# Layer 0 with six combined chunks, tile 2's chunks all behind them, and tile 1's pooling not held

## The chip, the cores and the metric

The kernel runs on one core of a Trainium2 chip. TensorE multiplies matrices, VectorE and ScalarE work element by element, and SyncE (SP) issues nearly all DMA transfers. The metric is the time of one execution on the device, in microseconds; a lower one is better.

## What is computed

One step of a streaming encoder of two layers, for a prompt of 1024 frames and a sample of 32 frames that share the weights, all in 32-bit floating point. Of the reference this matters here:

```python
for i in range(DEPTH):                                   # DEPTH = 2
    mod = jax.nn.silu(c) @ w_ada[i] + b_ada[i]
    sh1, sc1, gt1, sh2, sc2, gt2 = jnp.split(mod[:, None, :], N_MOD, axis=-1)
    h = rmsnorm(x, g_norm[i, 0]) * (1 + sc1) + sh1
    ...                                                  # layer 0: gated MLP, layer 1: pooling over time
    x = x + gt1 * rmsnorm(mix, g_norm[i, 1])
    h = rmsnorm(x, g_norm[i, 2]) * (1 + sc2) + sh2
    f = jnp.square(jax.nn.relu(h @ ffn_w_up[i])) @ ffn_w_down[i]
    x = x + gt2 * rmsnorm(f, g_norm[i, 3])
```

`ffn_w_up` is 1024 x 4096 and `ffn_w_down` 4096 x 1024 in each layer.

## The kernel before

**Tiles and chunks.** The 1056 frames are three tiles: tiles 0 and 1 of 384 frames, and tile 2 of 256 frames of the prompt and the 32 of the sample. The channel MLP of a layer is cut into eight chunks of 512 hidden channels. For one chunk and one tile (a tile-chunk) there are four up products of 24 matmuls and eight down products of 12: each product runs as three matmuls, high times high, high times low and low times high, because weights and activations are split into a high and a low part. A weight arrives through one of three raw buffers (`RAW_SLOTS`), 512 KB at a time; ScalarE makes its high part (line 436) and VectorE the low part.

**Passes.** The list `passes` (lines 322 to 333) sets the order: each entry names a layer, a chunk, and the tiles that use the weights loaded for it. In layer 0 it is: chunks 6 and 7 on tile 0; chunk 0 on tiles 0 and 1; chunk 1 on tile 0; chunk 1 on tile 1; chunks 2 to 5 combined; chunks 6 and 7 on tiles 1 and 2; chunks 0 to 5 on tile 2. In layer 1 it is: chunks 0 to 2 on tile 0; chunk 3 on tiles 0 and 1; chunks 0 to 2 on tile 1; chunks 4 to 7 combined; all eight chunks on tile 2.

**Combined chunks.** `combined_item` treats tiles 0 and 1 together and needs seven products in place of eight for a block of two by two up products. For that it uses sums and differences of the weights (`do_s`, VectorE work on `scratch`, a part of tile 2's `acc`) and of the activations' columns (`sums_of_columns`). The latter run once for a layer, need the modulated rows of all three tiles stored (`md`) and keep their results in the places of tile 0's and tile 2's `hh` and `hl` and in free buffers. So tile 2 must be modulated before the combined run, gives up its places for the length of it, and gets its rows back at the end (`late_modulation`, line 1859: ScalarE writes `hh`, VectorE `hl`). Some of the borrowed pieces hold hidden activations until the last down product of the run.

**Fillers.** All that stands between the matrix products (norms, residuals, modulation, pooling) is written as generators in the list `fillers`, named `ffn0_t`, `ffn1_t` and so on. `weave` (line 744) puts steps of them between the products as long as a running estimate of VectorE's time is behind TensorE's; `pull` (line 715) takes the first of the first two fillers that is open. A step that yields True is sticky: the same filler goes on next. A step that yields a number closes its filler for so many microseconds of the estimate. `open_` (line 719) also keeps `ffn1_1`, tile 1's pooling, closed while `ffn1_0`, tile 0's, is still in the list. The pooling groups of one tile are tied by `yield g != 3` (line 2014). Before a tile's first chunk of a layer its filler is finished by force. The framework then orders the instructions of each engine by their dependencies and an estimate of its own.

**The conditioning weights.** `w_ada` comes in items of 512 KB in the same stream as the other weights. VectorE multiplies each by the conditioning vectors and adds up (`aa`), four instructions of 512 columns for an item, and after every fourth item transposes and reduces. `some_ada` sets how many items go behind each pass: 40 of them are spread over the MLP, 4 + 2 + 2 before the combined run of layer 0, 6 behind each of its four combined chunks, 4 + 2 behind tile 2's chunks 0 and 1, and 2 behind the first combined chunk of layer 1.

Of the kernel before, what the change touches and what calls it, by code (L numbers as in the profile page):

```python
# [26 lines left out]
TILES = [(0, 384, 0), (384, 384, 0), (768, 256, DEC)]  # L27
NT = len(TILES)
W_SLOTS = 16
COMBINED = [range(2, 6), range(4, 8)]  # L30
RAW_SLOTS = 3
WINDOWS = (2, 4, 8, 16)

# [2 lines left out]
def tile_stream_encoder_step(  # L36
# [137 lines left out]
    def t_x(name, shape):  # L174
        return small.tile(shape, F32, tag="x3", bufs=3, name=name)
# [110 lines left out]
    def w_chunk(n):  # L286
        l, c, _ = passes[n]
        if n in combined:
            for i in range(2):
                f0 = c * 512 + i * 256  # L290
                for q in range(2):
                    stream.append(
                        (
                            "s",
                            ("up", n, i, q),
                            ffn_w_up[l][q * 512 : (q + 1) * 512, f0 : f0 + 256].rearrange(
                                "(k p) f -> p k f", p=P
                            ),
                            (4, 256),
                        )  # L300
                    )
        for j in range(0 if n in combined else 4):
            f = 4 * c + j
            add_w(
                ("up", n, j),
                ffn_w_up[l][:, f * P : (f + 1) * P].rearrange("(k p) f -> p k f", p=P),
                (8, P),
            )
        for q in range(4):
            add_w(  # L310
                ("dn", n, q),
                ffn_w_down[l][c * 512 : (c + 1) * 512, q * 256 : (q + 1) * 256].rearrange(
                    "(j p) d -> p j d", p=P
                ),
                (4, 256),
            )
# [3 lines left out]
    every = list(range(NT))  # L320
    pair = every[:-1]
    passes = []
    runs = []
    for l, cs in enumerate(COMBINED):
        before = [[(l, c, [0]) for c in (6, 7)] + [(l, 0, pair), (l, 1, [0]), (l, 1, [1])]]
        before.append([(l, c, [0]) for c in range(3)] + [(l, 3, pair)])
        before[1] += [(l, c, [1]) for c in range(3)]
        after = [[(l, c, every[1:]) for c in (6, 7)] + [(l, c, [NT - 1]) for c in range(6)]]
        after.append([(l, c, [NT - 1]) for c in range(8)])
        passes += before[l]  # L330
        runs.append(range(len(passes), len(passes) + len(cs)))
        passes += [(l, c, pair) for c in cs]
        passes += after[l]
# [9 lines left out]
    combined = [n for r in runs for n in r]  # L343
# [3 lines left out]
    def some_ada(n):  # L347
        for _ in range(min(n, len(rest))):
            add, l, j = rest.pop(0)
            add(l, j)  # L350
# [27 lines left out]
    for n, (l, c, tiles) in enumerate(passes):  # L378
        w_chunk(n)
        if n in combined:  # L380
            some_ada(2 if l else 6)
        elif l == 0 and c < 2:
            some_ada(4 if c == 0 else 2)
    assert not rest

    worder = [s[1] for s in stream if s[0] in "ws"]
# [323 lines left out]
    fillers = deque()  # L710
# [4 lines left out]
    def pull(force=False):  # L715

        def open_(f):
            if f[0] == "ffn1_1" and not force and any(g[0] == "ffn1_0" for g in fillers):  # L720
                return False
            return force or gates.get(f[0], 0.0) <= time["pe"]

        if sticky:
            f = sticky[-1]
            if not open_(f):
                return False
            sticky.pop()
        else:
            f = next((f for f in list(fillers)[:2] if open_(f)), None)  # L730
            if f is None:
                return False
        try:
            step = next(f[1])
        except StopIteration:
            fillers.remove(f)
            return True
        if step is True:
            sticky.append(f)
        elif step is not False:  # L740
            gates[f[0]] = max(time["pe"], time["dve"]) + step
        return True
# [1151 lines left out]
    def to_pool(st):  # L1894
        t = st.t
        n = ncol[t]
        npr, nsm = TILES[t][1], TILES[t][2]

        def run():
# [70 lines left out]
            for src, w, dst0, nm in parts:  # L1970
                for g in range(4):
                    cur = src[:, 2 * g : 2 * g + 2, :]
                    lo = 0
                    step = 1
                    for lev in range(g + 1):
                        nxt = t_x(f"win{t}{nm}{g}_{lev}", [P, 2, HALO + w])
                        lo += step
                        tt(
                            out=nxt[:, :, lo:],
                            in0=cur[:, :, lo:],  # L1980
                            in1=cur[:, :, lo - step : HALO + w - step],
                            op=ALU.add,
                        )
                        cur = nxt
                        step *= 2
                        yield True
                    body = cur[:, :, HALO:]
                    hsrc = src[:, 2 * g : 2 * g + 2, HALO:]
                    dst = acc[t][:, 2 * g : 2 * g + 2, HALO + dst0 : HALO + dst0 + w]
                    win = WINDOWS[g]  # L1990
                    first = t == 0
                    if first:
                        tt(
                            out=cur[:, :, HALO : HALO + win],
                            in0=cur[:, :, HALO : HALO + win],
                            in1=inv[:, 0:win].unsqueeze(1).broadcast_to([P, 2, win]),
                            op=ALU.mult,
                        )
                        tt(
                            out=dst[:, :, 0:win],  # L2000
                            in0=cur[:, :, HALO : HALO + win],
                            in1=hsrc[:, :, 0:win],
                            op=ALU.subtract,
                        )
                    o = win if first else 0
                    stt(
                        out=dst[:, :, o:],
                        in0=body[:, :, o:],
                        scalar=1.0 / win,
                        in1=hsrc[:, :, o:],  # L2010
                        op0=ALU.mult,
                        op1=ALU.subtract,
                    )
                    yield g != 3

            sp = Stat(t, f"rp_{t}")
            for g in range(4):
# [17 lines left out]
            yield from mix_to_ffn(sp, 1)  # L2035

        fillers.append((f"ffn1_{t}", run()))

    def run_ffn(l, after):
# [135 lines left out]
```

## Time and profile before

| | |
|---|---|
| median of 3 runs | 2147.0 us (2145.63 to 2147.81) |
| the profiled execution | 2145.2 us, span 2143.4 us |
| granted TensorE clock, mean | 0.999 |
| TensorE, matmuls / weight loads | 99% / 95% of the span busy |
| VectorE / ScalarE | 72% / 47% busy |
| channel MLP of layer 0 | 619 to 1365 us |
| combined run of layer 0 / of layer 1 | 834.7 to 1090.9 us / 1668.7 to 1921.5 us |

The page divides the span by engine, by slice and by line; TensorE's weight loads (PEld) overlap its matmuls (PE). The windows view gives the busy time of each engine in a stretch, with the number of instructions in brackets, then the granted clock (PEclk), the share of the DMA engines and their rate. Waits are put down to what came last.

### The profile page before, as it was taken

How to read it: one execution, taken by the hardware profiler on the slowest of the kernel's cores; microseconds unless marked ns; L12 is line 12 of the kernel's file. 1: busy time of each engine (PE TensorE's matmuls, PEld its weight loads, DVE VectorE, ACT ScalarE, POOL GpSimd, SP SyncE). 2: the span in 40 equal slices, each digit the busy share in tenths (PEclk: the TensorE clock that was granted, in tenths of full speed). 3: DMA queues.
4: the chain of work that ended last, by engine and by line, in shares of the span. 5: the costliest groups of instructions: out<-in, count | busy, mean ns of one | idle time of the engine just before them, and what ended most of it. 6: DMA issues, size and time to landing. Idle time of an engine off the chain costs nothing.

```text
span 2143.4 us, 33175 instructions
## 1 busy us (share of the span) xinstructions
PE 2120.2 (99%) x13041; PEld 2043.8 (95%) x13041; DVE 1533.1 (72%) x2786; ACT 1011.7 (47%) x1772; POOL 15.3 (1%) x34
## 2 busy tenths in 40 slices
PE   9999999999999999999999999999999999999998
PEld 6778999999999999999999999999999999999998
DVE  6787747466878668897778778969578654578464
ACT  5534322233456255244545556665355443365454
POOL 0000000000000000000000000000000000001000
PEclk9999999999999999999999999999999999999999
DMA  8487524353537454343434576665265322158662
GB/s 309 147 264 211 167 85 128 93 156 103 171 98 239 129 157 131 109 128 118 157 110 132 162 213 201 194 189 169 85 192 156 99 70 59 55 160 232 149 202 77
DMA packets 366002, 321.88 MB, mean 150 GB/s; under 512 B 39731, under 2 KB 328027, under 8 KB 365845
## 3 DMA queue, kind: packets, MB, share of 16 engines
q1 hardware_dynamic: 365172, 318.87, 48.8%
q8 instruction: 102, 1.67, 0.3%
q0 software_dynamic: 640, 0.88, 0.1%
q14 instruction: 56, 0.45, 0.1%
q10 hardware_dynamic: 32, 0.01, 0.0%
HBM read 279.22 MB, written 40.49 MB: 149 GB/s over the span
## 4 chain that ended last, share of the span: by engine, by line
PE 87%; DVE 5%; DMA 5%; ACT 2%; issue 1%; SPq 0%; DVEq 0%; ACTq 0%
PE pg L947 10%; PE pg L946 10%; PE pg L948 10%; PE pf L946 6%; PE pf L947 6%; PE pf L948 6%; PE pf_0a L1610 3%; PE po L947 3%; PE po L946 3%; PE po L948 3%; PE pu L946 3%; PE pu L948 3%; PE pu L947 3%; PE pv L974 2%; PE pv L973 2%; PE pv L975 2%
## 5 line engine op out<-in xcount | busy, mean ns | idle before, releaser
L946 PE MATMUL pg<-fh,wh_dn 128*128 128x384 f32 (+1 forms) x1344 | 431.6, 322 | 1.3 <-ACT fh L1359 1.1
L947 PE MATMUL pg<-fl,wh_dn 128*128 128x384 f32 (+1 forms) x1344 | 428.5, 319 | 0.9 <-DVE fl L80 0.9
L948 PE MATMUL pg<-fh,wl_dn 128*128 128x384 f32 (+1 forms) x1344 | 428.2, 319 | 0.0
L946 PE MATMUL pf<-hh,wh_up 128*128 128x288 f32 (+1 forms) x1024 | 323.2, 316 | 3.8 <-ACT wh_up L436 2.6
L947 PE MATMUL pf<-hl,wh_up 128*128 128x288 f32 (+1 forms) x1024 | 321.9, 315 | 0.8 <-DVE hl L80 0.8
L948 PE MATMUL pf<-hh,wl_up 128*128 128x288 f32 (+1 forms) x1024 | 322.1, 315 | 0.0
L946 PEld LDWEIGHTS pg<-fh,wh_dn 128*128 128x128 f32 x1344 | 252.1, 188 | 5.0 <-ACT fh L1359 3.4
L947 PEld LDWEIGHTS pg<-fl,wh_dn 128*128 128x128 f32 x1344 | 252.2, 188 | 2.2 <-DVE fl L80 1.1
L948 PEld LDWEIGHTS pg<-fh,wl_dn 128*128 128x128 f32 x1344 | 252.2, 188 | 0.0
L80 DVE TENSOR_TENSOR acc<-acc,pg 128x384 f32<-128x384 f32 (+1 forms) x336 | 172.4, 517 | 86.2 <-PE pg L948 85.3
L80 DVE TENSOR_TENSOR wl_dn<-raw,wh_dn 128x1024 fp32r<-128x1024 f32 x144 | 175.8, 1221 | 64.9 <-ACT wh_dn L436 60.3
L80 DVE TENSOR_TENSOR wl_up<-raw,wh_up 128x1024 fp32r<-128x1024 f32 (+1 forms) x160 | 160.3, 1008 | 77.6 <-ACT wh_up L436 66.3
L80 DVE SCALAR_TENSOR_TENSOR aa<-raw,csil,aa 128x512 f32<-128x512 f32 (+1 forms) x364 | 205.8, 624 | 11.6 <-DMA raw<-in_w_ada_dram 11.5
L436 ACT ACTIVATE wh_dn<-raw 128x1024 fp32r<-128x1024 f32 x144 | 151.4, 1055 | 96.8 <-PE pg L947 48.3
L946 PEld LDWEIGHTS pf<-hh,wh_up 128*128 128x128 f32 x1024 | 192.0, 188 | 5.0 <-ACT wh_up L436 3.1
L947 PEld LDWEIGHTS pf<-hl,wh_up 128*128 128x128 f32 x1024 | 192.2, 188 | 1.3 <-DVE hl L80 1.0
L948 PEld LDWEIGHTS pf<-hh,wl_up 128*128 128x128 f32 x1024 | 192.5, 188 | 0.3 <-DVE wl_up L80 0.2
L436 ACT ACTIVATE wh_up<-raw 128x1024 fp32r<-128x1024 f32 x112 | 118.3, 1058 | 134.9 <-PE pf L947 80.3
L946 PE MATMUL pu<-hh,wh_u 128*128 128x384 f32 (+1 forms) x384 | 125.8, 328 | 0.0
L946 PE MATMUL po<-ush,wh_o 128*128 128x384 f32 (+1 forms) x384 | 123.6, 322 | 0.0
L948 PE MATMUL pu<-hh,wl_u 128*128 128x384 f32 (+1 forms) x384 | 123.4, 321 | 0.0
L947 PE MATMUL pu<-hl,wh_u 128*128 128x384 f32 (+1 forms) x384 | 123.3, 321 | 0.0
(453 smaller groups left out, 4130.5 us busy)
## 6 DMA issues: line engine op xcount, KB each, us to landing
raw<-in_ffn_w_up_dram SPq DMA_DIRECT2D x144, 512.0 KB, 4.4
raw<-in_ffn_w_down_dram SPq DMA_DIRECT2D x144, 512.0 KB, 3.6
raw<-in_w_ada_dram SPq DMA_DIRECT2D x96, 512.0 KB, 4.7
raw<-in_sgu_w_in_dram SPq DMA_DIRECT2D x40, 512.0 KB, 4.2
xd<-acc SPq DMA_DIRECT2D x8, 1536.0 KB, 7.6
raw<-in_sgu_w_out_dram SPq DMA_DIRECT2D x24, 512.0 KB, 3.9
xo_r<-xd SPq DMA_DIRECT2D x32, 384.0 KB, 3.4
vd<-vt SPq DMA_DIRECT2D x32, 256.0 KB, 4.4
```

What stands on the lines that cost most here:

```text
L80: return op(out, *args, **kw)
L436: act(out=wh, in_=r, func=AF.Copy)
L946: mm(ps[:, :n], wh, rh, start=i == 0, stop=False)
L947: mm(ps[:, :n], wh, rl, start=False, stop=False)
L948: mm(ps[:, :n], wl, rh, start=False, stop=i == last)
L973: mm(ps[:m, :], a_h, wh[:, o : o + 512], start=k == 0, stop=False)
L974: mm(ps[:m, :], a_h, wl[:, o : o + 512], start=False, stop=False)
L975: mm(ps[:m, :], a_l, wh[:, o : o + 512], start=False, stop=k == KB - 1)
L1610: mm(ps[:, :n], u, v, start=first and k == 0 and x == 0, stop=k == 3 and x == 2, skip_group_check=True,)
```

## The change

Layer 0's combined run becomes chunks 2 to 7, six chunks. Ahead of it stand chunks 0 and 1 on tile 0, then chunks 0 and 1 on tile 1, each a pass with weights of its own: four tile-chunks where there were six. Behind it stand all eight chunks of tile 2, so tiles 0 and 1 both end with the combined run. There is one pass more (18 for 17). The `w_ada` items go 6 behind each of the first five combined chunks of layer 0, 2 behind the sixth, and 2 behind each of the four combined chunks of layer 1; none stands elsewhere in the MLP. Tile 1's pooling is no longer kept closed while tile 0's goes on, and a tile's pooling groups are no longer tied together.

```diff
-COMBINED = [range(2, 6), range(4, 8)]
+COMBINED = [range(2, 8), range(4, 8)]
...
-        before = [[(l, c, [0]) for c in (6, 7)] + [(l, 0, pair), (l, 1, [0]), (l, 1, [1])]]
+        before = [[(l, c, [t]) for t in pair for c in (0, 1)]]
...
-        after = [[(l, c, every[1:]) for c in (6, 7)] + [(l, c, [NT - 1]) for c in range(6)]]
+        after = [[(l, c, [NT - 1]) for c in range(8)]]
...
         if n in combined:
-            some_ada(2 if l else 6)
-        elif l == 0 and c < 2:
-            some_ada(4 if c == 0 else 2)
+            some_ada(2 if l else 6 if n + 1 in combined else 2)
...
         def open_(f):
-            if f[0] == "ffn1_1" and not force and any(g[0] == "ffn1_0" for g in fillers):
-                return False
             return force or gates.get(f[0], 0.0) <= time["pe"]
...
-                    yield g != 3
+                    yield False
```

## The prediction

> **What bounds the kernel now.** I read the page first.
>
> ```profile
> span 2143.4 us, 33175 instructions
> PE 2120.2 (99%) x13041; PEld 2043.8 (95%) x13041; DVE 1533.1 (72%) x2786; ACT 1011.7 (47%) x1772; POOL 15.3 (1%) x34
> PE 87%; DVE 5%; DMA 5%; ACT 2%; issue 1%; SPq 0%; DVEq 0%; ACTq 0%
> ```
>
> TensorE works nearly throughout and carries 87% of the chain that ended last. Fewer matmuls therefore shorten the run, unless something makes them wait. The question is what each removed matmul costs now, and which waits come in its place. So next I cut the span into its stages with the windows view: one stretch of two ordinary tile-chunks, the four combined chunks of layer 0, and the second and third combined chunk of layer 1.
>
> ```profile
> core 0: us, PE busy (x) PEld busy (x) DVE busy (x) ACT busy (x) POOL busy (x), PEclk, DMA share, GB/s
> 704.00:771.00 67.00, 67.00 (x389) 67.00 (x388) 42.37 (x72) 25.11 (x43) 0.00 (x0) 1.00 0.45 135
> 834.60:899.00 64.40, 63.63 (x368) 62.55 (x369) 54.94 (x101) 26.81 (x47) 0.00 (x0) 1.00 0.39 122
> 899.00:962.30 63.30, 63.30 (x370) 62.53 (x369) 52.26 (x92) 26.02 (x46) 0.00 (x0) 1.00 0.35 110
> 962.30:1027.20 64.90, 63.93 (x370) 62.62 (x369) 52.38 (x95) 26.02 (x46) 0.00 (x0) 1.00 0.39 122
> 1027.20:1090.90 63.70, 63.40 (x362) 62.44 (x361) 49.14 (x80) 33.17 (x66) 0.00 (x0) 1.00 0.50 156
> 1732.70:1795.40 62.70, 62.70 (x362) 62.44 (x361) 34.42 (x63) 25.11 (x46) 0.00 (x0) 1.00 0.23 68
> 1795.40:1858.20 62.80, 62.80 (x362) 62.54 (x361) 34.52 (x64) 25.11 (x46) 0.00 (x0) 1.00 0.23 68
> ```
>
> In the first row weight loads fill the whole stretch: 388 in 67.00 us, 172.7 ns for each 384-wide matmul. So I measure lost time in a row as its length less its PEld time: 1.85, 0.77, 2.28 and 1.26 us in layer 0's combined chunks, 6.16 together, but 0.26 and 0.26 in layer 1's. The matmul column hides most of that, since one matmul's end overlaps the next. The Trainium skill says so too: by Perfetto Trace Analysis, Identifying the Most-Contended Engine, matmul busy time is a poor measure and weight-load time a better one. The rows agree; by the matmul column the same four losses would be 0.77, 0, 0.97 and 0.30 us, 2.0 together, and the forecast below would come out about 2 us lower.
>
> **Part 1: fewer products.** An ordinary chunk on tiles 0 and 1 takes 2 x (96 + 96) = 384 matmuls. A combined one has 14 up products of 12 and 192 down matmuls, 360. Two more chunks become combined: 48 matmuls x 172.7 ns = **-8.3 us**. Tile 2's matmuls are the same ones in another order.
>
> **Part 2: what the combined chunks lose.** Layer 0's differ from layer 1's second and third in their six w_ada items each, whose multiply-adds (aa) go to VectorE. I take 0.26 us as a chunk's own loss; the rest, 6.16 - 1.04 = 5.1 us over 24 items, is 0.21 us an item. Two chunks are added (+0.5), and the combined chunks of both layers now carry 32 + 8 = 40 items where they carried 24 + 2: 14 x 0.21 = 3.0. Together **+3.5 us**, between 0.5 (the items are hidden) and 5.9 (both new chunks at 2.28, and 0.21 for six more items in layer 1).
>
> **Part 3: the stage of tile 2.** Those items leave two other places. One is tile 2's chunks, where six were loaded. The views: windows, PE's waits from 1197 to 1279, and VectorE's groups from 1217 to 1264.
>
> ```profile
> 1197.50:1279.00 81.50, 78.74 (x587) 77.81 (x586) 70.64 (x107) 45.38 (x71) 0.00 (x0) 1.00 0.69 213
> 1279.00:1364.90 85.90, 85.90 (x649) 85.90 (x649) 74.48 (x115) 55.80 (x93) 0.00 (x0) 1.00 0.70 212
> 1941.00:2082.00 141.00, 140.97 (x1054) 139.69 (x1054) 93.45 (x135) 71.57 (x115) 9.95 (x16) 1.00 0.70 189
> ```
> ```profile
> PE pf L946 <- ACT wh_up L436: 2.6, 2, 2.0
> ```
> ```profile
> L80 DVE SCALAR_TENSOR_TENSOR aa<-raw,csil,aa 128x512 f32<-128x512 f32 x20 | 14.0, 749 | 0.2 <-DMA raw<-in_w_ada_dram 0.2
> L80 DVE TENSOR_SCALAR aa<-raw,csil 128x512 f32<-128x512 f32 x4 | 1.9, 483 | 0.0
> L80 DVE TENSOR_TENSOR wl_up<-raw,wh_up 128x1024 fp32r<-128x1024 f32 x5 | 6.1, 1218 | 2.3 <-ACT wh_up L436 2.3
> ```
>
> The six items take 15.9 us of VectorE and hold the three raw buffers through which the weights also come; 3.69 us are lost (81.50 - 77.81), 2.6 of them waiting for an up weight. The next stretch has no such item and loses nothing, with VectorE busy 87%. After the change the stage has no item, but the pooling of two tiles at once. I let it lose what layer 1's tile-2 stage does, 1.3 us: **-2.4 us**, between -3.7 and, if VectorE cannot keep up, rival 2. SP's queue, the one that loads the weights, also reloads the residual rows (xo) there, and one such issue held it for up to 9.6 us:
>
> ```profile
> SPq L859 <- DVE acc L80: 22.4, 6, 9.6
> ```
>
> Tile 1's reloads now come into the same stage; layer 1's row includes such reloads for two tiles, and its 1.3 us are what they cost. The two edits of the order (tile 1's pooling not held, the pooling groups no longer tied together) issue nothing of their own; what they can do is rival 2. The one more pass of weights (eight splits of 1.22 us on VectorE, eight 512 KB loads) I cost at nothing: it lies under matmuls, like the six such passes now in this stage; without that cover it would be 9.8 us of VectorE, part of rival 2.
>
> **Part 4: the new seam.** Now layer 0's combined run is followed by tile 1's chunk 6, and tile 2's low parts (hl) are written under it. After the change tile 2's first product comes at once, as it does in layer 1 already:
>
> ```profile
> 1090.90:1128.00 37.10, 37.10 (x228) 36.82 (x227) 25.32 (x50) 15.12 (x25) 0.00 (x0) 1.00 0.33 99
> 1921.50:1941.00 19.50, 17.19 (x126) 16.61 (x125) 19.50 (x40) 10.76 (x20) 0.00 (x0) 1.00 0.66 180
> ```
> ```profile
> PE pn_rf L839 <- ACT sc_rf L824: 1.5, 1, 1.5
> PE pf L947 <- DVE hl L80: 0.8, 1, 0.8
> ```
> ```profile
> 1922.03 4.56 DVE L80 SCALAR_TENSOR_TENSOR hl<-acc,shift,hh 128x256 fp32r<-128x256 f32 x16
> ```
>
> Layer 1's seam loses 2.89 us, layer 0's now 0.28: **+2.6 us**, between 0.5 (only the 0.8 us wait returns) and 2.6. The hl room can't be free earlier, because the last down products read pieces of it.
>
> **Part 5: the entry to the first combined chunk.** Six tile-chunks stand ahead of it now, four will. It needs tile 2's modulation, its store (md), the sums of columns, and its own first weights. The views: two rows by tile, the timeline, the windows, and VectorE's groups from 700 to 722.
>
> ```profile
> L1774 SPq DMA_DIRECT2D md<-acc x2: 526/545/564, 723.2 to 1595.0; - x2
> L80 DVE TENSOR_TENSOR sums_c<-sums_m,sums_l x2: 551/551/551, 822.3 to 1637.3; 128x384 fp32r<-128x384 f32 x2
> ```
> ```profile
> 780.27 0.61 ACT L1842 ACTIVATE hl<-acc,dshift 128x384 fp32r<-128x384 f32 x1
> 834.70 0.45 PE L1610 MATMUL pf_0a<-hh,wh_up 128*128 128x384 f32 x1
> ```
> ```profile
> 804.00:834.60 30.60, 29.48 (x177) 28.91 (x175) 28.79 (x53) 13.36 (x26) 0.00 (x0) 1.00 0.46 140
> ```
> ```profile
> L80 DVE SCALAR_TENSOR_TENSOR aa<-raw,csil,aa 128x512 f32<-128x512 f32 x14 | 9.7, 744 | 0.0
> L563 DVE STREAM_TRANSPOSE raw<-aa 128x512 f32<-128x512 f32 x2 | 1.4, 704 | 0.0
> L566 DVE TENSOR_REDUCE sums<-raw 128x32 f32<-128x1024 f32 x1 | 1.2, 1211 | 0.0
> ```
>
> Now the store goes at 723.2 and the sums end at 822.8 only because tile 0's last up product keeps their home in hh and hl until about 780; after the change that product ends two tile-chunks earlier. Layer 1, where the home is free, takes 1595.0 to 1637.8, 42.8 us. From the last sum to the first combined matmul are 11.9 us (822.8 to 834.7). The combined run could start two tile-chunks earlier, at 834.7 - 66.3 = 768.4. With the store at 723.2 the start would be 723.2 + 42.8 + 11.9 = 777.9, 9.5 us late. But 12.3 us of w_ada work sit among tile 2's modulation (9.7 + 1.4 + 1.2) and go elsewhere. With the store at 711 the start is 765.7, in time. The present entry loses 1.7 us (30.60 - 28.91), and I keep that: **0 us**, between -1.7 and +9.5 (rival 1).
>
> **The sum**: -8.3 + 3.5 - 2.4 + 2.6 + 0 = **-4.6 us**. The profiled execution took 2145.2 us (a span of 2143.4 and 1.8 around it), 1.8 below the median of the runs, 2147.0. So 2140.6 for such an execution, and 2142.4 us as a median.
>
> **Rival 1, slower: the sums come late.** If tile 2's modulation isn't earlier, TensorE stands at the first combined chunk for up to 9.5 us: -4.6 + 9.5 = +4.9, 2152 us. It decides from a store later than about 714 (768.4 - 42.8 - 11.9). For it: the present store at 723.2, and VectorE almost full in 804 to 834. Against it: the 12.3 us that go, and no w_ada item any more in that whole stretch. The Trainium skill has a rule that makes this dearer: by TensorE: Matmul & The Clock Gate, Part 1, an idle window of about 3.4 us halves TensorE's clock until it has been busy for as long, which by my estimate would add 1.7 us. No row here tests it: the longest wait shown is 2.0 us, and PEclk is 1.00 in every row.
>
> **Rival 2, slower: tile 0 isn't ready for layer 1.** The timeline has its steps.
>
> ```profile
> 1227.24 0.61 DVE L80 SCALAR_TENSOR_TENSOR sm_r_0x<-sq_r_0x,eps,sc_r_0x 128x384 fp32r<-128x384 f32 x1
> 1290.58 0.55 DVE L80 SCALAR_TENSOR_TENSOR q_r_0x<-pn_r_0x,q_r_0x 128x384 f32<-128x384 f32 x1
> 1310.65 0.61 DVE L80 SCALAR_TENSOR_TENSOR hl<-acc,shift,hh 128x384 fp32r<-128x384 f32 x1
> 1364.93 0.34 PE L946 MATMUL pf<-hh,wh_up 128*128 128x384 f32 x1
> ```
>
> From the end of the combined run (1090.9) tile 0's last low part takes until 1311.3, 220 us; layer 1 starts at 1364.9, 54 us later. Eight tile-2 chunks give 8 x 192 x 132.4 ns (85.9 us / 649) = 203 us. The present chain would be 17 us late. But it stands still for 63 us (1227.9 to 1290.6), behind the six items and the weights; without them it fits. If tile 1, no longer held back, takes that room, TensorE waits perhaps 10 us of the 17: -4.6 + 10 = +5.4, 2152 us.
>
> **Rival 3, faster: nothing is paid.** The moved items are hidden (part 2: 0.5), the tile-2 stage loses nothing (-3.7), the seam costs 0.5: -8.3 + 0.5 - 3.7 + 0.5 = -11, 2136 us.
>
> **How the numbers follow.** A measurement of this kernel tells 0.2% from no change, 4.3 us. The forecast has 0.5, with a range of its own from 2138 to 2147, half of it on either side of the 4.3 us; rival 1 has 0.2, rival 2 0.1, rival 3 0.2. Faster: 0.25 + 0.2 = 0.45; the same: 0.25; slower: 0.3. The range goes from 2137, just above rival 3, to 2154, rival 1 with 2 us for the clock or a second late wait.
>
> **What would show it.** Right: 360 weight loads in each of six combined chunks of 63 to 65 us; the store of tile 2's modulation by 714 and the run's start near 768; no up-weight wait in the tile-2 stage; 2 to 3 us lost at the seam; tile 0's last hl well ahead of layer 1's first matmul. Wrong: a PE wait of over 3 us at the entry or at layer 1's start, VectorE full through the tile-2 stage, or combined chunks over 66 us.

## The result, and the profile after

| | before | after |
|---|---|---|
| median, runs side by side | 2146.8 us | 2159.3 us |
| ratio, 95% interval | | 1.0056 (1.0044 to 1.0067) |
| profiled span | 2143.4 us | 2156.7 us |

The change makes the kernel 0.56% slower; the prediction was 2142.4 us, range 2137 to 2154. The head of the page after, and the chain's shares:

```profile
span 2156.7 us, 33207 instructions
PE 2121.3 (98%) x12993; PEld 2038.6 (95%) x12993; DVE 1564.4 (73%) x2854; ACT 1029.1 (48%) x1808; POOL 15.3 (1%) x34
PE 83%; DVE 7%; DMA 6%; ACT 3%; issue 1%; SPq 0%; DVEq 0%; ACTq 0%
```

The 48 matmuls are gone (12993 for 13041), yet the span is 13.3 us longer: the time went into waits. The windows view, by stage (columns as in the prediction): the six combined chunks of layer 0, the seam and the rest of tile 2's stage, the start of layer 1, and layer 1's four combined chunks.

```profile
769.00:833.30 64.30, 63.48 (x362) 62.30 (x361) 50.84 (x90) 26.18 (x46) 0.00 (x0) 1.00 0.37 115
833.30:896.70 63.40, 63.40 (x370) 62.59 (x369) 52.29 (x91) 26.01 (x46) 0.00 (x0) 1.00 0.36 111
896.70:961.50 64.80, 63.86 (x370) 62.54 (x369) 52.25 (x96) 26.02 (x46) 0.00 (x0) 1.00 0.40 122
961.50:1024.50 63.00, 62.97 (x362) 62.44 (x361) 51.93 (x89) 26.07 (x46) 0.00 (x0) 1.00 0.36 110
1024.50:1088.90 64.40, 63.81 (x370) 62.48 (x369) 52.10 (x95) 26.29 (x46) 0.00 (x0) 1.00 0.39 121
1088.90:1153.30 64.40, 63.60 (x370) 62.51 (x368) 45.21 (x72) 38.95 (x76) 0.00 (x0) 1.00 0.48 151
1153.30:1172.00 18.70, 17.18 (x132) 16.75 (x128) 14.29 (x33) 11.13 (x22) 0.00 (x0) 1.00 0.45 135
1172.00:1286.80 114.80, 114.80 (x868) 114.80 (x867) 102.94 (x153) 72.29 (x117) 0.00 (x0) 1.00 0.71 218
...
1371.80:1380.80 9.00, 1.65 (x5) 0.73 (x4) 9.00 (x15) 3.73 (x8) 0.00 (x0) 0.69 0.55 148
1380.80:1404.00 23.20, 23.14 (x120) 22.59 (x121) 15.22 (x23) 13.40 (x24) 0.00 (x0) 0.90 0.53 166
...
1675.20:1739.60 64.40, 63.24 (x362) 62.33 (x361) 39.02 (x71) 25.00 (x46) 0.00 (x0) 1.00 0.26 82
1739.60:1802.90 63.30, 63.06 (x362) 62.50 (x361) 41.63 (x74) 25.45 (x46) 0.00 (x0) 1.00 0.27 83
1802.90:1867.50 64.60, 63.33 (x362) 62.39 (x361) 39.10 (x71) 25.00 (x46) 0.00 (x0) 1.00 0.27 82
1867.50:1931.80 64.30, 63.42 (x370) 62.49 (x369) 45.47 (x73) 38.74 (x75) 0.00 (x0) 1.00 0.50 155
```

Read by length less PEld, as the prediction did: layer 0's six chunks lose 2.00, 0.81, 2.26, 0.56, 1.92, 1.89, together 9.4 us (6.2 in four before). Layer 1's lose 2.07, 0.80, 2.21, 1.81, together 6.9 us (2.4 before), although they carry two w_ada items each, where five of layer 0's carry six and the last two. And from 1371.8 to 1380.8 TensorE does next to nothing while VectorE is full. PE's waits from 1153.3 to 1404 name what ended that stretch:

```profile
PE pn_rf L835 <- ACT sc_rf L820: 4.6, 2, 3.1
PE pf L942 <- ACT hh L915: 4.2, 1, 4.2
```

The longest of the first (3.1 us) is tile 2's own norm, which has its place in PE's order ahead of layer 1. The second is layer 1's first product waiting for the high part (hh) of tile 0's modulated rows. The steps of tile 0 on VectorE, with three of tile 1's among them (timeline; win1p is tile 1's pooling), the pooling matmuls and the store of tile 2's modulation, used further down (rows by tile; the range at the end gives the first and the last start), and layer 1's first product on PE:

```profile
1171.02 0.55 DVE L80 SCALAR_TENSOR_TENSOR q_rf<-pn_rf,q_rf 128x384 f32<-128x384 f32 x1
...
1255.76 0.92 DVE L80 SCALAR_TENSOR_TENSOR acc<-win0p,acc 128x736 f32<-128x736 f32 x1
...
1264.56 2.61 DVE L80 TENSOR_TENSOR sq_r_1x<-sq_r_1x 128x768 f32<-128x768 f32 x3
...
1289.13 0.61 DVE L80 SCALAR_TENSOR_TENSOR sm_r_1x<-sq_r_1x,eps,sc_r_1x 128x384 fp32r<-128x384 f32 x1
...
1353.58 0.62 DVE L80 SCALAR_TENSOR_TENSOR sm_r_0x<-sq_r_0x,eps,sc_r_0x 128x384 fp32r<-128x384 f32 x1
...
1374.63 0.98 DVE L80 TENSOR_TENSOR win1p<-acc 128x798 f32<-128x798 f32 x1
...
1376.85 0.55 DVE L80 SCALAR_TENSOR_TENSOR q_r_0x<-pn_r_0x,q_r_0x 128x384 f32<-128x384 f32 x1
...
1387.81 1.15 DVE L80 SCALAR_TENSOR_TENSOR hl<-acc,shift,hh 128x384 fp32r<-128x384 f32 x2
```
```profile
L2025 PE MATMUL pp<-acc,wg x96: 404/485/486, 1299.6 to 1566.2; 128*128 128x384 f32 x64, 128*128 128x288 f32 x32
```
```profile
L1770 SPq DMA_DIRECT2D md<-acc x2: 525/544/563, 718.4 to 1609.2; - x2
```
```profile
1380.86 0.69 PE L942 MATMUL pf<-hh,wh_up 128*128 128x384 f32 x1 [4.16 <-ACT hh L915]
```

Tile 0's pooling windows end at 1256.7, but its pooling matmuls begin only at 1299.6, 43 us later; between them stands tile 1's second norm (sq_r_1x, sm_r_1x). Before, the same two steps were 7.6 us apart (1171.3 to 1178.9), and the pooling matmuls began 88 us after the end of the combined run; now it is 146 us (1153.3 to 1299.6). Tile 0's last low part ends at 1389.0, before at 1311.3. VectorE wasn't full through all of these 43 us, as the windows and PE's timeline show:

```profile
1268.00:1299.60 31.60, 31.60 (x240) 31.60 (x239) 19.40 (x27) 17.80 (x29) 0.00 (x0) 1.00 0.69 220
```
```profile
1299.63 0.81 PE L2025 MATMUL pp<-acc,wg 128*128 128x384 f32 x2
```

PE came to the pooling matmuls without a wait: they stood in its order behind tile 2's products. So in that stretch it was the place of tile 0's steps in the order of instructions, more than VectorE's time, that made them late. From 1340 to 1371.8 VectorE was full again (31.22 of 31.80 us).

Milestones of the two profiles, each with the tile-chunks that the change moves across it taken out:

| place | after against before |
|---|---|
| first combined matmul of layer 0 (769.0; 834.7 - 66.3) | +0.6 us |
| end of that run (1153.3; 1090.9 + 66.3) | -3.9 |
| last product of tile 2's stage (1371.8; 1381.6 - 24 up matmuls of layer 1, 4.1) | -5.7 |
| layer 1's products begin, tile 2's stage done on both sides (1380.9; 1377.5) | +3.4 |
| start, end of layer 1's combined run (1675.3; 1668.7) (1931.9; 1921.5) | +6.6, +10.4 |
| span | +13.3 |

### The profile page after: what moved, and what is told of

Its sections match the earlier page's. It is cut to its first block, busy times and chain, and to the rows that moved or that the text cites. A ratio compares the mean times of both kernels' runs of the same rounds, so it can differ in the third digit from the quotient of the medians.

```text
span 2156.7 us, 33207 instructions
## 1 busy us (share of the span) xinstructions
PE 2121.3 (98%) x12993; PEld 2038.6 (95%) x12993; DVE 1564.4 (73%) x2854; ACT 1029.1 (48%) x1808; POOL 15.3 (1%) x34
## 4 chain that ended last, share of the span: by engine, by line
PE 83%; DVE 7%; DMA 6%; ACT 3%; issue 1%; SPq 0%; DVEq 0%; ACTq 0%
PE pg L942 10%; PE pg L943 10%; PE pg L944 10%; PE pf L942 5%; PE pf L943 5%; PE pf L944 5%; PE pf_0a L1606 3%; PE po L942 3%; PE po L943 3%; PE po L944 3%; DMA raw<-in_w_ada_dram 3%; PE pu L942 3%; PE pu L944 3%; PE pu L943 3%; PE pv L969 2%; PE pv L970 2%
## 5 line engine op out<-in xcount | busy, mean ns | idle before, releaser
L942 PE MATMUL pg<-fh,wh_dn 128*128 128x384 f32 (+1 forms) x1296 | 415.7, 321 | 3.4 <-ACT fh L1355 2.6
L943 PE MATMUL pg<-fl,wh_dn 128*128 128x384 f32 (+1 forms) x1296 | 412.8, 319 | 0.2 <-DVE fl L80 0.2
L944 PE MATMUL pg<-fh,wl_dn 128*128 128x384 f32 (+1 forms) x1296 | 412.3, 318 | 0.1
L942 PE MATMUL pf<-hh,wh_up 128*128 128x288 f32 (+1 forms) x896 | 281.4, 316 | 5.9 <-ACT hh L915 4.2
L943 PE MATMUL pf<-hl,wh_up 128*128 128x288 f32 (+1 forms) x896 | 280.5, 314 | 0.1
L944 PE MATMUL pf<-hh,wl_up 128*128 128x288 f32 (+1 forms) x896 | 280.2, 313 | 0.2 <-DVE wl_up L80 0.2
L942 PEld LDWEIGHTS pg<-fh,wh_dn 128*128 128x128 f32 x1296 | 243.0, 188 | 7.2 <-ACT fh L1355 4.5
L942 PEld LDWEIGHTS pf<-hh,wh_up 128*128 128x128 f32 x896 | 169.1, 189 | 7.1 <-ACT hh L915 4.5
L943 PEld LDWEIGHTS pf<-hl,wh_up 128*128 128x128 f32 x896 | 169.3, 189 | 1.2 <-DVE hl L80 0.9
L944 PEld LDWEIGHTS pf<-hh,wl_up 128*128 128x128 f32 x896 | 169.7, 189 | 0.4 <-DVE wl_up L80 0.4
```

What stands on the lines that cost most here:

```text
L942: mm(ps[:, :n], wh, rh, start=i == 0, stop=False)
L943: mm(ps[:, :n], wh, rl, start=False, stop=False)
L944: mm(ps[:, :n], wl, rh, start=False, stop=i == last)
```

## The experiments

The theories: tile 0 isn't ready for layer 1 because tile 1's steps, no longer held, go between its own (A); the new place of tile 2's chunks costs tile 0 its slack, while the combined chunks bring about what was predicted (G); a combined chunk with any w_ada item loses a fixed amount (D). Rivals: VectorE's load whatever the order (B), the two edits of the order alone (C), a price per item (E), combined chunks that bring little (H), and combined chunks that cost as much in waits as they save (I).

**1. The hold and the tie back.** This run is in effect that of the hold alone: run 6 has the hold without the tie, and up to layer 1's combined run both traces have the same instructions in the same order on every engine.
```diff
+            if f[0] == "ffn1_1" and not force and any(g[0] == "ffn1_0" for g in fillers):
+                return False
...
-                    yield False
+                    yield g != 3
```


> The changed kernel with both edits of the order taken back (tile 1's pooling closed while tile 0's goes on, pooling groups tied). Theory A (order): tile 0 is late at layer 1's start because tile 1's steps go between its own; with the hold the 9 us in which TensorE stands from 1371.8 to 1380.8 and the half clock behind them (1380.8 to 1385.4, 2.3 us) go: 2147 to 2150 us, 9 to 12 below the changed kernel's 2159. Rival B (load): with both tiles ending together at the end of the combined run, VectorE has too much to do in tile 2's stage whatever the order; tile 0's last low part still comes after 1365 us and the time stays within 3 us of 2159.

2151.6 us, ratio 1.0028 (1.0016 to 1.0040). By the two ratios 6 us come back, by the medians 7.7: the direction of theory A, short of its 9 to 12. (Four of the six executions took 2150.6 to 2151.6 us, two 2156.8 and 2157.5; what made these two longer isn't known.) The timeline shows tile 0's last low part and layer 1's first product:
```profile
1356.53 0.61 DVE L80 SCALAR_TENSOR_TENSOR hl<-acc,shift,hh 128x384 fp32r<-128x384 f32 x1
```
```profile
1362.49 0.34 PE L944 MATMUL pf<-hh,wh_up 128*128 128x384 f32 x1
```
Tile 0 is ready 5 us ahead, with no wait, so rival B falls as it stood. But before it was ready 54 us ahead, and the kernel is still slower than that one: the hold is not the whole cause.

**2. The two edits of the order alone, in the kernel before.**
```diff
-            if f[0] == "ffn1_1" and not force and any(g[0] == "ffn1_0" for g in fillers):
-                return False
...
-                    yield g != 3
+                    yield False
```


> The kernel before with only the two edits of the order. Theory A: tile 1's pooling takes VectorE from tile 0's here too, though tile 1 comes two tile-chunks later (66 us): tile 0 had 54 us to spare at layer 1's start, so the time stays within 4 us of 2147, and tile 0's last low part moves from 1311 to between 1330 and 1365. Rival C (the two edits alone are what costs): 2155 us or more.

2147.2 us, ratio 0.9997 (0.9988 to 1.0006): they cost nothing there, and rival C falls. Tile 0's last low part moves from 1311 only to 1315, less than I had expected. The edits hurt only together with the new order of the chunks.

**3. The move of the items alone, in the kernel before.**
```diff
         if n in combined:
             some_ada(2 if l else 6)
-        elif l == 0 and c < 2:
+        elif l == 0 and c < 2 and n < runs[0][0]:
             some_ada(4 if c == 0 else 2)
```


> The kernel before with only the move of six w_ada items from tile 2's chunks 0 and 1 into layer 1's second to fourth combined chunk, two each. Theory D (a chunk with items loses about 1.5 us more than one without, however many they are): layer 1's combined run loses 3.5 to 4.5 us more, tile 2's stage 2.4 less: 2148 to 2149 us. Rival E (0.21 us an item, as the prediction had it; layer 1's losses follow from the late start): layer 1's run +1.3, tile 2's stage -2.4: 2146 us or less.

2148.5 us, ratio 1.0006 (0.9997 to 1.0015): no difference that the measurement tells, though the profile's stages do. Tile 2's stage from 1197.5 to 1279, which lost 3.69 us before, and layer 1's last two combined chunks (windows):
```profile
1197.50:1279.00 81.50, 81.39 (x612) 81.16 (x611) 71.48 (x111) 52.58 (x86) 0.00 (x0) 1.00 0.69 211
...
1795.00:1860.00 65.00, 63.90 (x366) 62.97 (x365) 39.70 (x72) 25.36 (x47) 0.00 (x0) 1.00 0.27 82
1860.00:1922.80 62.80, 62.00 (x360) 60.90 (x359) 43.59 (x69) 37.82 (x74) 0.00 (x0) 1.00 0.52 155
```
The stage now loses 0.34 us; the two chunks lose 2.0 and 1.9, before 0.26 and 0.43. Layer 1's run is 256.8 us long (252.8 before), and the stage behind it 216.6 us (214.8). That bears out theory D. The trace answers one more question. The prediction said that tile 0's chain stood still for 63 us behind the six items; with the items gone it stands for 6, and its last low part comes at 1257.3, 54 us earlier than before:
```profile
1256.69 0.61 DVE L80 SCALAR_TENSOR_TENSOR hl<-acc,shift,hh 128x384 fp32r<-128x384 f32 x1
```

**4. No item in layer 1, in the kernel after.**
```diff
-            some_ada(2 if l else 6 if n + 1 in combined else 2)
+            some_ada(0 if l else 7 if n - runs[0][0] < 4 else 6)
```


> The changed kernel with no w_ada item in layer 1's combined run: seven behind each of the first four combined chunks of layer 0, six behind the other two. Theory D: layer 1's run gets 3.5 to 4.5 us back and layer 0's loses 0 to 1.5 more: 2155 to 2157 us. Rival E: the items cost the same in either run: 2159 us, within 1.

2180.3 us, ratio 1.0155 (1.0141 to 1.0169): a miss for both theories, and a test of another kind. The six items of the last chunk stood in front of tile 0's first steps (24 multiply-adds from 1110 to 1140; 8 before 1118 after the change). Tile 0's first norm and its pooling slid by 57 and 62 us, and TensorE stood for 21 us:
```profile
1227.65 0.55 DVE L80 SCALAR_TENSOR_TENSOR q_rf<-pn_rf,q_rf 128x384 f32<-128x384 f32 x1
```
```profile
L2025 PE MATMUL pp<-acc,wg x96: 403/486/561, 1362.0 to 1624.3; 128*128 128x384 f32 x64, 128*128 128x288 f32 x32
```
```profile
PE pn_r_0x L835 <- ACT sc_r_0x L820: 15.0, 1, 15.0
PE pf L942 <- ACT hh L915: 3.1, 1, 3.1
PE pn_rp L835 <- ACT sc_rp L820: 2.8, 1, 2.8
```
With four items more at that place, 16 multiply-adds or 12 us of VectorE, tile 0's pooling came 62 us late. VectorE didn't lack the time for tile 0's steps, since it was busy for only 33.55 of the first 53 us behind the run:
```profile
1153.00:1206.00 53.00, 49.76 (x365) 48.53 (x365) 33.55 (x54) 32.63 (x57) 0.00 (x0) 1.00 0.62 182
```
The steps stood late in the order of instructions: on ScalarE the first one (r_rf) ran at 1155.4, and the next (q_rf) at 1225.9, without a wait before it. `weave` places them by its running estimate of VectorE's time; that a lag of this estimate turned 12 us into 57 is likely, but no run shows it. Between the end of the combined run and layer 1 the changed kernel has no slack.

**5. Four combined chunks as before, but all of tile 2's chunks behind them, with the hold.**
```diff
-        before = [[(l, c, [0]) for c in (6, 7)] + [(l, 0, pair), (l, 1, [0]), (l, 1, [1])]]
+        before = [[(l, c, [0]) for c in (6, 7)] + [(l, 0, pair), (l, 1, [0]), (l, 1, [1])] + [(l, c, [1]) for c in (6, 7)]]
...
-        after = [[(l, c, every[1:]) for c in (6, 7)] + [(l, c, [NT - 1]) for c in range(6)]]
+        after = [[(l, c, [NT - 1]) for c in range(8)]]
...
-            some_ada(2 if l else 6)
-        elif l == 0 and c < 2:
+            some_ada(2 if l or n + 1 not in combined else 6)
+        elif l == 0 and n < runs[0][0] and (c < 2 or tiles == [1]):
             some_ada(4 if c == 0 else 2)
```


> The kernel before with its four combined chunks, but all eight chunks of tile 2 behind them and so eight tile-chunks of tiles 0 and 1 ahead (one pass of weights more); w_ada items out of tile 2's stage as in the changed kernel; tile 1's pooling held as before. It differs from the run with the hold (2151.6) only in that chunks 6 and 7 aren't combined, and from the kernel before with the items moved (2148.5) only in where tile 1's last two chunks stand. Theory G (the two combined chunks bring what the prediction said, 8.3 less some 3; the place of tile 2's chunks costs what tile 0 loses in slack): 2156 to 2158 us, 5 above the run with the hold and 8 above the one with the items moved. Rival H (the place costs nothing, as the prediction's parts 3 and 4 had it, and the combined chunks bring little): 2149 to 2152 us.

2156.9 us, ratio 1.0042 (1.0029 to 1.0054). Theory G, and rival H falls: the new place of tile 2's chunks, with its one more pass of weights, costs 8.4 us even with the hold (2156.9 against 2148.5; by the two ratios 7.7), and two more combined chunks bring 5.3 (2151.6 against 2156.9; the spans, 2149.8 and 2155.1, say the same). Neither comparison is quite clean, since the items ahead of the run and in it differ too: 12 and 20 here, 8 and 24 in run 3, none and 32 in run 1. Tile 0 isn't late here: its last low part ends at 1360.5, layer 1's first product comes at 1365.6, and PE waits for nothing there. Part of the cost is waits for tile 1 (PE's waits from 1420 to 1670; in run 3 these two were 0.3 and 0.4 us):
```profile
PE pp L2029 <- DMA wg<-in_pool_w_grp_dram: 3.0, 1, 3.0
PE pg L946 <- ACT fh L1359: 1.4, 1, 1.4
```

**6. The items at the front of layer 1's run.** Layer 1's eight items 4 + 4 behind its first two combined chunks, in the changed kernel with the hold:
```diff
-            some_ada(2 if l else 6 if n + 1 in combined else 2)
+            some_ada((4 if n < runs[1][0] + 2 else 0) if l else 6 if n + 1 in combined else 2)
```


> The changed kernel with the hold, and layer 1's eight w_ada items 4 + 4 behind its first two combined chunks in place of 2 behind each. Theory D (a chunk with items loses a fixed 1.3 to 1.8 us, and items in the last one delay the first steps of tile 0's output and cost 2 us more behind the run): 4 to 5 us below the run with the hold, 2147 us. Rival E (a price per item): the same as the run with the hold, 2151.6, within 1.

2150.0 us, ratio 1.0007 (0.9999 to 1.0016), 1.6 below the run with the hold: nearer rival E's 2151.6 than theory D's 2147, as a wait of 2.4 us for pooling weights at 1557 was 0.8 longer here and a stretch at half clock followed it. The chunks themselves are as theory D has them:
```profile
1661.40:1733.00 71.60, 70.73 (x404) 69.69 (x404) 54.42 (x99) 29.29 (x52) 0.00 (x0) 1.00 0.31 96
1733.00:1799.00 66.00, 65.33 (x379) 64.02 (x378) 48.06 (x87) 25.79 (x46) 0.00 (x0) 1.00 0.32 97
1799.00:1863.00 64.00, 64.00 (x369) 63.74 (x369) 35.67 (x66) 25.15 (x46) 0.00 (x0) 1.00 0.23 71
1863.00:1926.40 63.40, 63.40 (x365) 62.95 (x364) 39.66 (x63) 40.02 (x77) 0.00 (x0) 1.00 0.47 139
```
With four items a chunk loses 1.9 and 2.0 us, no more than with two; without any 0.26 and 0.45. By the chunks, if not by the time, rival E falls; run 10 repeats it with the time on the same side.

**7. The items ahead of that run**, on tile 1's single passes (the diff adds `elif l and n < runs[1][0] and tiles == [1]: some_ada(2)` and leaves 2 behind the first combined chunk):

> The changed kernel with the hold, and layer 1's eight w_ada items 2 behind each of tile 1's three passes ahead of the combined run and 2 behind the first combined chunk. Theory D: layer 1's second to fourth combined chunk lose 0.26 us each again and the stage behind them 2 us less; 146 to 148 us over 2000, unless the items delay tile 2's modulation, which would show as a wait at layer 1's first combined chunk of 1 to 6 us. Rival E: 2151.6, within 1.

2152.5 us, ratio 1.0017 (1.0008 to 1.0026). By the time alone this is rival E's forecast. But the second to fourth chunk lose 0.26, 0.26 and 0.45 us again; a wait of 2.6 us for fh stands at the entry, as the exception had it, and with the half clock behind it (0.83 from 1655 to 1665) it eats the gain.

**8. Five combined chunks**, with the kernel before's order behind them (hold and tie as before, the items placed as the expectation says):
```diff
-COMBINED = [range(2, 6), range(4, 8)]
+COMBINED = [range(3, 8), range(4, 8)]
...
+        before = [[(l, c, [0]) for c in (1, 2, 0)] + [(l, 0, [1])]]
...
+        after = [[(l, c, every[1:]) for c in (1, 2)] + [(l, c, [NT - 1]) for c in (0, 3, 4, 5, 6, 7)]]
```


> The kernel before with chunks 3 to 7 combined: chunks 1, 2 and 0 on tile 0 and chunk 0 on tile 1 ahead; chunks 1 and 2 on tiles 1 and 2 behind, as chunks 6 and 7 were; then tile 2's other six; w_ada items 6 behind each combined chunk, 1, 1, 4, 2 behind the next four passes, 2 in layer 1. Theory G: the order behind the run, which gave tile 0 its slack, is kept; one chunk brings -4.15 us and loses 0.8 to 2: 2144 to 2145 us. Rival I (any combined chunk more costs as much in waits as it saves): 2147 us or more.

2149.4 us, ratio 1.0009 (1.0000 to 1.0017): not the gain that theory G gave, but rival I's 2147 or more. The entry waits 2.5 us for fh and tile 2's stage 2.3 us for an activation, each followed by a stretch at half clock.

**9. The same with the items out of that stage** and 4 + 4 in layer 1 (`some_ada((4 if n < runs[1][0] + 2 else 0) if l else 6)`, and 1 behind each of the two passes on tiles 1 and 2):

> Five combined chunks as in the earlier run (2149.4), with layer 1's items 4 + 4 behind its first two combined chunks and none in tile 2's stage. The earlier run's wait of 2.3 us in that stage and the 3.4 us of half clock behind it (1.7 us) go, layer 1's second combined chunk loses 1.7 more: 2146 to 2148 us, the first version that would come down to the kernel before. If the wait at 752 us (2.5 us, and half clock) is what costs, it stays at 2149.

2146.9 us, ratio 0.9992 (0.9983 to 1.0001). The second wait goes, the first stays (2.6 us), so the fifth chunk brings nothing that can be told; run 10, beside it on the same chip, is 1.7 us lower by the median with four, though the two intervals overlap.

**10. The same placing of the items in the kernel before**, with nothing else changed:
```diff
-            some_ada(2 if l else 6)
-        elif l == 0 and c < 2:
+            some_ada((4 if n < runs[1][0] + 2 else 0) if l else 6)
+        elif l == 0 and n < runs[0][0] and c < 2:
             some_ada(4 if c == 0 else 2)
```

> The kernel before with tile 2's stage of layer 0 free of w_ada items and layer 1's eight items 4 + 4 behind its first two combined chunks. If a chunk with items loses a fixed amount: layer 1's second combined chunk +1.7, its first unchanged, the tile-2 stage -2.4: 2146 to 2147 us, 1 to 2 below the run with the items 2 behind each of four. With a price per item: as that run, 2148.5.

2145.2 us, ratio 0.9984 (0.9975 to 0.9993): the one version whose interval lies below the kernel before, 0.16% faster, by moving six items and nothing else. That is theory D again: the second combined chunk of layer 1, with four items, loses 1.93 us, the third, with none, 0.26:
```profile
1729.00:1793.00 64.00, 63.39 (x367) 62.07 (x366) 46.09 (x83) 25.83 (x46) 0.00 (x0) 1.00 0.32 98
1793.00:1857.00 64.00, 64.00 (x369) 63.74 (x368) 35.58 (x67) 25.15 (x46) 0.00 (x0) 1.00 0.23 72
```

**11. TensorE kept busy in the wait.** The changed kernel with 44 matmuls of ones ahead of layer 1's first product, their result unused:
```diff
+                    late0 = l == 1 and t == 0 and any(f[0] == "ffn1_0" for f in fillers)
                     finish(f"ffn{l}_{t}")
+                    if late0:
+                        keep = ps_up("keep")
+                        for _ in range(44):
+                            mm(keep[:, :384]..., onesr, ..., start=True, stop=True)
```


> The changed kernel with 44 idle-time matmuls (ones by ones, 384 wide, 7.6 us) just ahead of layer 1's first product, where TensorE stood for 9.1 us; nothing else is changed. If the 10 us at half clock behind that wait come from the wait, the granted clock stays 1.0 there and the first 120 up products take 20.7 us in place of 23.1: 2.3 us less, 2157 us. If the clock has another cause, the time is the same, 2159.3.

2157.5 us, ratio 1.0044 (1.0031 to 1.0058); its interval overlaps that of the changed kernel, and the profiled spans, 2155.8 and 2156.7 us, differ by 0.9, so the time alone doesn't tell. The windows do:
```profile
1372.20:1381.50 9.30, 8.36 (x50) 8.12 (x48) 9.30 (x15) 3.62 (x8) 0.00 (x0) 1.00 0.54 148
1381.50:1404.20 22.70, 21.85 (x120) 20.78 (x121) 14.95 (x23) 13.24 (x24) 0.00 (x0) 1.00 0.50 168
```
The granted clock stays 1.00 (0.69 and 0.90 in the changed kernel), so the wait was what halved it. But the 120 matmuls take 22.7 us for 23.2, not 20.7, probably because the low parts of tile 0 were still coming (the last ends at 1389.0 in the changed kernel). I had put 2.3 us down to the half clock there; 0.5 of it was.

## Why the prediction was wrong, point by point

The forecast was -4.6 us, and the profiled span grew by 13.3. Of these 17.9 us, 9.3 arise at layer 1's start, 3.2 in the products up to layer 1's combined run, and 5.4 in and behind that run (the table of milestones). The step that failed first is in rival 2: that tile 0's chain, 220 us less 63 of standing still, so 157, fits into the 203 us behind the combined run. It took 236 us. The second is the size of part 2's term for layer 1: 1.3 us, for which 7 came.

**Part 1 held** (48 matmuls fewer; the combined chunks bring 5.3 us for two by run 5, where parts 1 and 2 for layer 0 give 8.3 - 2.2 = 6.1).

**Part 2 failed in its form.** I spread the losses of layer 0's chunks over the items, 0.21 us each. Runs 3, 6 and 10 show a cost of a chunk that has any: 0.6 to 2.3 us with two, four or six, and 0.26 to 0.45 with none. So the three chunks of layer 1 that got two items each cost about 4 us, not 1.3. The stage behind the run is 217.9 us long for 214.8 (3.4 us at half clock from 2102.2 among them). It took 216.6 us in run 3, with items in the last chunk too, and 214.8 and 215.9 in runs 4 and 6, with none there; so part of its growth goes with the items of the last chunk. Together 7 us for 1.3.

**Parts 3, 4 and 5 held in the waits that they name, not in a term that part 3 put at nothing.** Tile 2's stage lost its up-weight waits (run 3: 3.69 to 0.34). The seam loses 1.95 us; 1.7 more than before, 2.6 were taken. The store of tile 2's modulation goes at 718.4, later than the 714 that I had set as the limit, but the run starts at 769.0: the way from the store to the run took 50.6 us, not the 54.7 read from layer 1. Rival 1 did not occur. At the last product of tile 2's stage the change was 5.7 us ahead; the forecast's parts come to 5.9 there. That agreement is partly luck: the combined run brought 4.5 us where 6.1 were forecast, and tile 2's stage 1.8 where parts 3 and 4 together cost 0.2. The term at nothing is the extra pass of weights, which I took to lie under matmuls. Run 5 prices it together with the new place of tile 2's chunks: 8 us, even with the hold. How much of that is the pass isn't shown; and since tile 0 isn't late in run 5, these 8 us don't come from TensorE waiting for tile 0.

**Rival 2 is what happened, and its chance of 0.1 was far too low.** Of the three signs of a wrong forecast one came, a wait of over 3 us at layer 1's start, and a second in part: VectorE was 90% full from 1172.0 to 1286.8, but not all through the stage. The wait's price was near: I said 10 us; 9.0 us without a product of the MLP came, and 2.5 more on the 120 matmuls behind them (23.2 us, 20.7 at full pace). Of this, too, part is luck. The 17 us by which the old chain would be late came out (tile 0's last low part ends at 1389.0, tile 2's stage at 1371.8), but with both numbers off: the chain took 236 us, not 220, and the stage 218.5, not 203.

The low chance came from taking tile 0's chain from the trace of before, 220 us less the 63, so 157 us, as if it would run as fast in its new place. In us from the end of the combined run of layer 0:

| tile 0 | before | items moved out (run 3) | changed, with the hold (run 1) | after |
|---|---|---|---|---|
| pooling windows end | 80 | 81 | 94 | 103 |
| first pooling matmul | 88 | 88 | 116 | 146 |
| last low part ends | 220 | 166 | 204 | 236 |

The items were rightly read: without them the old order takes 166 us. But the new place adds 38 us even with the hold (run 5, with the hold and four combined chunks, has 203 too), and taking the hold away adds 32 more. Before, the first 88 us lay beside chunks 6 and 7 on tiles 1 and 2, where VectorE was busy 65.94 us; now they lie beside tile 2 alone, where eight weight splits come every 25 us instead of every 59, and VectorE is busy 78.88 us:

```profile
1090.90:1179.00 88.10, 88.10 (x567) 87.82 (x566) 65.94 (x112) 45.11 (x80) 0.00 (x0) 1.00 0.39 118
1153.30:1241.50 88.20, 86.68 (x656) 86.25 (x652) 78.88 (x129) 58.46 (x100) 0.00 (x0) 1.00 0.63 191
```

(The first row is the kernel before, from the end of its run to tile 0's pooling matmuls; the second is the same length after.) VectorE's load is one reason; the order of the instructions is another, as the 43 us before tile 0's pooling matmuls and run 4 show. In time, taking the hold away costs 6 to 8 us here (run 1) and nothing in the old order (run 2).

**The clock.** The Trainium skill's rule (TensorE: Matmul & The Clock Gate, Part 1: an idle window of about 3.4 us halves the clock until TensorE has been busy as long) now has its rows: 0.69 and 0.90 above, and 1.00 in the same place when TensorE was kept busy. By run 11 it cost 0.5 us there, less than the 1.7 that I had estimated for one such stretch, probably because the products were waiting for tile 0's low parts anyway.

What stays open: how the 8.4 us of run 5 divide between the extra pass, the seam, tile 1's late pooling and the half-clock stretches (no run takes one away alone), and how much of the 38 us is VectorE's load and how much the order.

## What to carry to other kernels

A product saved on the engine that bounds is worth what its stage had to spare: before moving passes, take the length of every chain that must end by a given point, and the busy share of its engines, from a trace with the new neighbours, not from the old one. Where background work delays its host by a wait, ask whether the cost is per host stage or per item; here it was per stage, so the items belong in few stages and not in the last one. An edit that costs nothing alone (taking the hold away) can be decisive once another edit has used up the slack.

## What the runs showed of the hardware

Short waits can halve the clock, but not each does. In the run with the hold one wait of 1.8 us at 1160.5, for an activation, was followed by 3.4 us at half clock, which shows in a 10 us window as a granted clock of 0.83:

```profile
PE pf L944 <- ACT r L1532: 1.8, 1, 1.8
```
```profile
1160.00:1170.00 10.00, 8.19 (x50) 7.95 (x49) 5.54 (x9) 5.73 (x12) 0.00 (x0) 0.83 0.53 159
```

The 3.4 us of idleness that the Trainium skill gives (TensorE: Matmul & The Clock Gate, Part 1) were thus not needed here, and the measurement decides. The 2.0 us wait in the kernel before had no such stretch: the row of its stage in the prediction has 1.00. In the change's 9 us wait the half clock began some 3 us after the wait did and lasted 10.2 us (1375.2 to 1385.4), three times 3.4, with 4.6 of them behind the wait; in run 4, with 21 us of waiting, the granted clock was 0.54 over the 20 us from 1377. A stretch of 3.4 us at half clock can cost up to 1.7 us (half of it); whether its coming and going is why executions of one kernel differ by a few microseconds was not tested.
